# Two up-projection loads moved ahead of four modulation loads, and twelve PSUM copies moved from VectorE to ScalarE

## The chip, the cores and the metric

The kernel runs on one core of a Trainium2 chip. The metric is the device time of one execution in microseconds (us); it is the median over several executions of the same program. The engines are TensorE (PE in the rows; its weight loads are PEld), VectorE (DVE), ScalarE (ACT), GpSimd (POOL) and SyncE (SP), whose only work here is to issue DMAs.

## What is computed

The whole program is a mixer block followed by two transformer layers over 256 tokens of 1024 features, in fp32. The change lies in the first layer's attention, a latent attention with 8 heads, and touches the modulation that runs beside it. Cut to that:

```python
mod = (silu(c) @ mod_w[i] + mod_b[i]).reshape(B, 6, D)     # six rows of 1024 per layer
hin = x * (1.0 + mod[:, 1]) + mod[:, 0]

proj = hin @ w_in                                           # 1024 -> 576
c_q  = rms_norm(proj[..., :256], q_norm)
c_kv = rms_norm(proj[..., 256:512], kv_norm)
k_rope = apply_rope(proj[..., 512:], cos, sin)
q  = (c_q  @ w_uq ).reshape(B, S, 8, 192)                   # 128 plain + 64 rotary each
kv = (c_kv @ w_ukv).reshape(B, S, 8, 256)                   # 128 keys + 128 values each
q = concat([q[..., :128], apply_rope(q[..., 128:], cos, sin)])
k = concat([kv[..., :128], broadcast(k_rope)])
o = causal_softmax_attention(q, k, kv[..., 128:], 192 ** -0.5)
y = merge_heads(o) @ w_o
```

## The kernel before

Every large matmul is done in three passes: a weight `w` and an activation `x` are each split into a rounded part and a rest (`wh`, `wl`, `xh`, `xl`), and `wh*xh + wh*xl + wl*xh` accumulates in PSUM. `split` makes the two parts of a weight: a CAST on ScalarE (line 174) and a subtraction on VectorE (line 175). All weights stream from HBM through one pool of six tiles named `raw` (8 KB in each partition); a load can be issued only when one of the six is free again, and all loads are issued by SP in one order.

The attention function `mla` runs so. `tokens` and `halves` multiply the 256 tokens by `w_in` (tiles `ps_lat`, weights `lat0` to `lat7`), in two blocks of 128 tokens. `done(tb)` then normalises the 256+256 latents of a block: squares on ScalarE (`lsq`), a reciprocal square root on GpSimd (`lr`), two scalings on VectorE (`lt`, lines 1206 and 1207), five transposes on TensorE (`ltT`, `ltR`), and the split of the transposed latents into `ck` and `cq`, ScalarE and VectorE by turns. `units(0)` and `units(1)` are the up-projections, four heads each: a load of 1 MB of `w_ukv` (`raw_ukv`), four loads of together 768 KB of `w_uq` (`raw_uq`), the splits of both, the values (`ps_mlv`), the keys (`ps_kn`), the rotary part of the queries (`ps_qr`, then `rope`) and the plain part (`ps_qn`). The second half runs in pieces between the heads (`fill`). The three PSUM tiles of the tag "M" are used in turn by `ltT`, `ltR`, `mlv`, `kn`, `qr` and `qn`, so a tile that is copied out late holds up a later matmul.

The modulation is a queue of 48 load-and-multiply units of 1 MB each (`raw_mod`, `ps_mod`), four to a row of `mod`, with a closing step after each four that reads the sum (`modr`), transposes it (`modt`) and copies it out (`mod`). `halves` fetches `fill` units ahead of time and multiplies them after its own matmuls, while the normalisation runs. All units of a row share one PSUM tile (tag "V"), and the next row's can start only after the closing copy. In this attention the two last units of row 2 of the first layer's modulation and the four of the next row come up; the program's names for them are `mod044`, `mod046`, `mod030`, `mod032`, `mod034`, `mod036`.

What each engine does in which order is decided when the program is built: a scheduler orders the instructions of each engine by a model of their times, and the order is fixed from then on. Each engine runs its own list strictly in order and waits at semaphores.

Of the kernel before, what the change touches and what calls it, by code (L numbers as in the profile page):

```python
# [13 lines left out]
ALU = mybir.AluOpType  # L14
# [4 lines left out]
P = 128  # L19
S = 256  # L20
# [27 lines left out]
class G:  # L48
# [202 lines left out]
            for tb in range(2):  # L251
                self.nc.scalar.copy(out[tb][:, c:c + 512], pst[tb])

    def halves(self, load, ks, x, acc, width, name, ends, done=None, fill=0, by_column=False):

        ws = {}
        for i, k in enumerate(ks):
            with ExitStack() as ctx:  # L260
                if k != ends[0]:
                    self.after_marks(ctx)
                ws[k] = self.split(load(k), f"{name}{k}", i >= NW)
        self.fetch(fill)
        orders = []
        for tb in range(2):
            cols = list(enumerate(width[tb]))
            late = ks if by_column and tb else ks[-2:]
            orders.append([(k, n, c) for k in ks[:-len(late)] for n, c in cols] + [(k, n, c) for n, c in cols for k in late])
        ins = None  # L270
        for tb in range(2):
            t = slice(tb * P, (tb + 1) * P)
            with nullcontext() if ins is None or done is None else self.tc.issue_after(ins.ins):
                for k, n, c in orders[tb]:
                    wh, wl = ws[k]
                    ins = self.mm3t(acc(tb, n), x[k][0][:, t], x[k][1][:, t], wh[:, c], wl[:, c], k == ends[0], k == ends[1])
            if tb == 0:
                self.flush()
            if done is not None and tb == 0:
                done(0)  # L280
        if fill:
            with self.tc.issue_after(ins.ins):
                self.units(fill)
        if done is not None:
            self.pending = lambda: done(1)

    def tokens(self, w, x, groups, acc, done, name, c0=0, width=None, fill=0, by_column=False):

        width = (N512, TAIL) if by_column else (width or N512,) * 2
        load = self.loader(w, c0, width[0][-1].stop, name)  # L290
        for ks in groups:
            end = (done, fill, by_column) if ks is groups[-1] else ()
            self.halves(load, ks, x, acc, width, name, (groups[0][0], groups[-1][-1]), *end)

    def loader(self, w, c0, n, name):
# [892 lines left out]
def mla(g, x, ln, early):  # L1188
    nc, a = g.nc, g.a
    V, A, T = nc.vector, nc.scalar, nc.tensor  # L1190
    w = a["mla_w_in_2"][0]
    cuts = [slice(0, 256), slice(256, 576)]
# [4 lines left out]
    def done(tb):  # L1197
# [22 lines left out]
            V.scalar_tensor_tensor(l_[:, t], o, w_, h_[:, t].bitcast(F32), op0=ALU.mult, op1=ALU.subtract)  # L1220
        A.copy(kx[:, t], p2[:, 0:P])

    acc = lambda tb, n: lacc(tb, n, (256, 320)[n])
    g.tokens(w, x, [[0, 1, 2, 3], [4, 5, 6, 7]], acc, done, "lat", width=cuts, fill=6)
    g.flush()
    rest = early()

    def rope(src, name):
        ps = g.ps(name + "rp", "A")
        T.matmul(ps[:, 0:S], g.perm, src, start=True, stop=True)  # L1230
        t, u = g.t1(name + "rc"), g.t1(name + "rs")
        nc.gpsimd.tensor_tensor(t, src, g.trig[0], op=ALU.mult)
        V.tensor_tensor(u, ps[:, 0:S], g.trig[1], op=ALU.mult)
        nc.gpsimd.tensor_tensor(t, t, u, op=ALU.add)
        return t


    krr = rope(kx, "kr")
    kr = [g.t1(f"krz{e}") for e in range(2)]
    for e in range(2):  # L1240
# [5 lines left out]
    kn, qn = g.quad("kn0", F32) + g.quad("kn1", F32), g.quad("qn0", F32) + g.quad("qn1", F32)  # L1246

    def units(hf):
        rv = g.wload(a["mla_w_ukv_2"][0], 0, 2, 1024 * hf, 1024, f"ukv{hf}")
        raw = g.raw(f"uq{hf}")[:, 0:2 * 768].rearrange("p (k c) -> p k c", k=2)  # L1250
        for k in range(2):
            src = a["mla_w_uq_2"][0][k * P:(k + 1) * P, 768 * hf:768 * hf + 768].rearrange("p (h c) -> p h c", h=4)
            nc.sync.dma_start(raw[:, k, 0:512].rearrange("p (h c) -> p h c", h=4), src[:, :, 0:P])
            nc.sync.dma_start(raw[:, k, 512:768].rearrange("p (h c) -> p h c", h=4), src[:, :, P:192])
        with ExitStack() as ctx:
            if hf == 0:
                g.after_marks(ctx)
            ws = [g.split(rv[:, k, :], f"ukv{hf}{k}") for k in range(2)]
        wv = [[t.rearrange("p (h c) -> p h c", h=4) for t in w_] for w_ in ws]
        pv = [g.ps(f"mlv{hf}{tb}", "M") for tb in range(2)]  # L1260
        for tb in range(2):
            for k in range(2):
                t = slice(tb * P, (tb + 1) * P)
                o = pv[tb].rearrange("p (h c) -> p h c", h=4)
                g.mm3t(o, ck[k][0][:, t], ck[k][1][:, t], wv[k][0][:, :, P:S], wv[k][1][:, :, P:S], k == 0, k == 1)
            A.copy(vt[tb][:, 512 * hf:512 * hf + 512], pv[tb])
            yield
        for hh in range(4):
            h = 4 * hf + hh
            ps = g.ps(f"kn{h}", "M")  # L1270
            for k in range(2):
                g.mm3(ps[:, 0:S], wv[k][0][:, hh, 0:P], wv[k][1][:, hh, 0:P], *ck[k], k == 0, k == 1)
            A.copy(kn[h], ps[:, 0:S])
            yield
        with ExitStack() as ctx:
            if hf == 0:
                g.after_marks(ctx)
            wq = [g.split(raw[:, k, :], f"uq{hf}{k}") for k in range(2)]
        for pr in range(2):
            ps = g.ps(f"qr{hf}{pr}", "M")  # L1280
            for k in range(2):
                h_, l_ = (t[:, 512 + P * pr:512 + P * pr + P] for t in wq[k])
                g.mm3(ps[:, 0:S], h_, l_, *cq[k], k == 0, k == 1)
            xq = g.t1(f"qrx{hf}{pr}")
            V.tensor_copy(xq, ps[:, 0:S])
            yield
            qr[2 * hf + pr] = rope(xq, f"qr{hf}{pr}")
            for e in range(2):
                hh = 2 * pr + e
                h = 4 * hf + hh  # L1290
                ps = g.ps(f"qn{h}", "M")
                for k in range(2):
                    h_, l_ = (t[:, hh * P:hh * P + P] for t in wq[k])
                    g.mm3(ps[:, 0:S], h_, l_, *cq[k], k == 0, k == 1)
                ins = V.tensor_copy(qn[h], ps[:, 0:S])
                if hf and rest:
                    rest.pop(0)(ins)
                yield

    for _ in units(0):  # L1300
        pass
    later = units(1)

    def fill(st):
# [11 lines left out]
    n, done = ln()  # L1316
    acc = g.pair("mlay")
# [147 lines left out]
def program(tc, a, out):  # L1465
    with ExitStack() as ctx:
        g = G(ctx, tc, a)
        g.out = out
        g.wk = ctx.enter_context(tc.tile_pool(name="wk", bufs=1))
        h, hl, pw = block1(g)  # L1470
        n = gated(g, h, hl, pw)
        for i in range(2):
            def mid(i=i, n=n):
                g.bg_to(i, 3)
                return resid_ln(g, i, 0, n.r, (g.mod[i][4], g.mod[i][3]), f"ln{i}0")

            n = (mla, moba)[i](g, n.x, mid, n.residual)

            def end(i=i, n=n):
                g.bg_to(i, 5)  # L1480
                if i == 0:
                    g.bg_to(1, 0)
                    return resid_ln(g, 0, 1, n.r, (g.mod[1][1], g.mod[1][0]), "ln01")
                return None, last_ln(g, n.r)

            n = ffn(g, i, n.x, end, n.residual)
        g.flush()
# [32 lines left out]
```

## Time and profile before

| | |
|---|---|
| median of 3 runs | 877.22 us (877.14 to 877.37) |
| the profiled execution's own time | 879.18 us |
| its span, first to last instruction | 877.4 us |
| TensorE busy | 859.3 us, 98% of the span |
| VectorE busy / ScalarE busy | 673.2 us / 502.6 us |
| HBM traffic over the span | 226 GB/s |
| latent attention up to its output projection | about 270 to 343 us after the start |

The time of the profiled execution lies 1.8 us above its span, and the median of the runs 2.0 us below it; differences between stages are read in the span. A row of the timeline gives the start, the length, the engine, the line, the operation with its output and input tiles, how many instructions were merged, and in brackets how long the engine stood idle before it and whom it waited for. A length of a matmul includes its drain, so matmuls follow each other faster than their lengths.

### The profile page before, as it was taken

The numbers are of one execution on the slowest core, as the hardware profiler recorded it, in microseconds if no ns is written. First come the engines' busy times: TensorE is split into PE (matmuls) and PEld (weight loads), VectorE is DVE, ScalarE is ACT, GpSimd is POOL, SyncE is SP. The second block draws the span as 40 slices with busy tenths as digits, with TensorE's granted clock in tenths as the row PEclk, the third lists the DMA queues.
The fourth block names the chain that finished last, engine by engine and source line by source line (L and its number), as shares of the span: only waits on it lengthen the run. The fifth ranks groups of instructions, "written<-read, shape, count | busy, mean of one in ns | idle before, by whom it ended". The sixth has DMA issues, their size and how long they took to land. (4 is left out here: it accounts for less than half of the span.)

```text
span 877.4 us, 14288 instructions
## 1 busy us (share of the span) xinstructions
PE 859.3 (98%) x5415; PEld 741.1 (84%) x5415; DVE 673.2 (77%) x1289; ACT 502.6 (57%) x925; POOL 52.6 (6%) x81
## 2 busy tenths in 40 slices
PE   9999999999999899999999999999999999999996
PEld 8998779999888688798888888678888988888885
DVE  5798787768767576679899998675866686777786
ACT  6555666445557555377556557276553775565660
POOL 2003111000000131000000000000000000000003
PEclk9999999999999999999999999999999999999999
DMA  8955796854447963498898985498453956566411
GB/s 269 357 197 175 279 345 202 285 211 151 144 150 258 305 250 117 132 377 286 305 331 296 336 290 190 162 345 296 161 176 104 377 178 203 181 220 204 143 49 48
DMA packets 112760, 199.27 MB, mean 227 GB/s; under 512 B 8388, under 2 KB 76468, under 8 KB 112692
## 3 DMA queue, kind: packets, MB, share of 16 engines
q1 hardware_dynamic: 111892, 196.25, 65.7%
q0 software_dynamic: 496, 1.59, 0.5%
q8 instruction: 42, 0.69, 0.3%
q10 hardware_dynamic: 304, 0.53, 0.2%
q14 instruction: 26, 0.21, 0.1%
HBM read 197.28 MB, written 1.08 MB: 226 GB/s over the span
## 5 line engine op out<-in xcount | busy, mean ns | idle before, releaser
L194 PE MATMUL ps_f<-ln,wh_f 128*128 128x512 f32 x576 | 203.8, 396 | 0.0
L195 PE MATMUL ps_f<-ln,wl_f 128*128 128x256 f32 x576 | 161.4, 280 | 0.0
L194 PEld LDWEIGHTS ps_f<-ln,wh_f 128*128 128x128 f32 x576 | 108.1, 188 | 26.5 <-issue 0.8
L195 PEld LDWEIGHTS ps_f<-ln,wl_f 128*128 128x128 f32 x576 | 108.7, 189 | 1.4 <-issue 0.4
L174 ACT CAST wh_fo<-raw_fo 128x1024 fp32r<-128x1024 f32 x38 | 39.9, 1050 | 39.3 <-PE ps_f L194 38.2
L174 ACT CAST wh_f<-raw_fa 128x1024 fp32r<-128x1024 f32 x36 | 37.7, 1051 | 40.8 <-PE ps_f L194 20.3
L175 DVE TENSOR_TENSOR wl_fo<-raw_fo,wh_fo 128x1024 fp32r<-128x1024 f32 x38 | 46.5, 1223 | 19.0 <-ACT wh_fo L174 18.9
L175 DVE TENSOR_TENSOR wl_f<-raw_fa,wh_f 128x1024 fp32r<-128x1024 f32 x36 | 43.9, 1222 | 15.3 <-ACT wh_f L174 15.3
L174 ACT CAST wh_f<-raw_fb 128x1024 fp32r<-128x1024 f32 x36 | 37.1, 1050 | 28.0 <-PE ps_fy L215 17.8
L998 DVE SCALAR_TENSOR_TENSOR modacc<-raw_mod,c,modacc 128x1024 f32<-128x1024 f32 x40 | 51.1, 1278 | 2.0 <-ACT modacc L996 2.0
L175 DVE TENSOR_TENSOR wl_f<-raw_fb,wh_f 128x1024 fp32r<-128x1024 f32 x36 | 43.4, 1221 | 9.2 <-ACT wh_f L174 8.9
L188 PE MATMUL ps_fi<-ln,wh_fi 128*128 128x256 f32 x128 | 35.6, 285 | 0.0
L215 PE MATMUL ps_fy<-wh_fo,fh 128*128 128x512 f32 (+1 forms) x99 | 35.2, 369 | 0.0
L214 PE MATMUL ps_fy<-wl_fo,fh 128*128 128x512 f32 (+1 forms) x99 | 35.1, 368 | 0.0
L189 PE MATMUL ps_fi<-ln,wl_fi 128*128 128x256 f32 x128 | 34.6, 283 | 0.0
L187 PE MATMUL ps_fi<-ln,wh_fi 128*128 128x256 f32 x128 | 34.0, 286 | 0.0
L213 PE MATMUL ps_fy<-wh_fo,fh 128*128 128x512 f32 (+1 forms) x99 | 33.3, 367 | 0.0
L204 DVE TENSOR_TENSOR adf<-ps_f,adf 128x256 f32<-128x256 f32 x72 | 30.0, 417 | 0.0
L983 PE MATMUL ps_mod<-raw_mod,c 128*32 128x256 f32 x400 | 26.9, 383 | 1.0 <-DVE mod L1013 1.0
L203 ACT COPY adf<-ps_f 128x256 f32<-128x256 f32 x72 | 26.1, 363 | 0.0
L174 ACT CAST wh_fi<-raw_fi 128x1024 fp32r<-128x1024 f32 x16 | 17.0, 1079 | 14.9 <-PE ps_mlay L215 8.3
L188 PEld LDWEIGHTS ps_fi<-ln,wh_fi 128*128 128x128 f32 x128 | 24.5, 192 | 0.4 <-DVE ln L377 0.4
(807 smaller groups left out, 2582.4 us busy)
## 6 DMA issues: line engine op xcount, KB each, us to landing
raw_mod<-in_mod_w_dram SPq DMA_DIRECT2D x48, 1024.0 KB
raw_fo<-in_ffn_w_out_dram SPq DMA_DIRECT2D x22, 1024.0 KB
raw_fa<-in_ffn_w_in_dram SPq DMA_DIRECT2D x18, 1024.0 KB
raw_fb<-in_ffn_w_in_dram SPq DMA_DIRECT2D x18, 1024.0 KB
raw_fi<-in_ffn_w_in_dram SPq DMA_DIRECT2D x16, 512.0 KB
raw_wo<-in_w_out_dram SPq DMA_DIRECT2D x6, 1024.0 KB
raw_aqk<-in_w_in_dram SPq DMA_DIRECT2D x4, 1024.0 KB
raw_mqk<-in_w_in_dram SPq DMA_DIRECT2D x4, 1024.0 KB
```

Source lines behind the costliest of these rows:

```text
L174: self.nc.scalar.copy(hv, src)
L175: self.nc.vector.tensor_tensor(lv, src, hv.bitcast(F32), op=ALU.subtract)
L187: T.matmul(ps, wh, xh, start=start, stop=False, skip_group_check=chk)
L188: T.matmul(ps, wh, xl, start=False, stop=False, skip_group_check=chk)
L189: T.matmul(ps, wl, xh, start=False, stop=stop, skip_group_check=chk)
L194: T.matmul(ps, wh, x[2], start=start, stop=False, skip_group_check=True)
L195: T.matmul(ps[:, 0:S], wl, x[0], start=False, stop=stop, skip_group_check=True)
L204: V.tensor_tensor(t, ps[:, 0:S], t, op=ALU.add)
L213: T.matmul(ps, xh, wh, start=start, stop=False)
L214: T.matmul(ps, xh, wl, start=False, stop=False)
L215: return T.matmul(ps, xl, wh, start=False, stop=stop)
L998: nc.vector.scalar_tensor_tensor(st["acc"], rv[:, e], c, st["acc"], op0=ALU.mult, op1=ALU.add)
```

## The change

Three edits. The loads of an up-projection half become a function `loads(hf)`; for half 0 it is called from inside `halves` (argument `pre`), after the input projection's own loads and ahead of the fetch of modulation units, so these two tiles stand earlier in SP's order. Four units are fetched and multiplied there (`fill=4`) where there were six; the other two of the row are asked for later by `fill`'s call of `bg`. And the query tiles, rotary (`qrx`) and plain (`qn`), are copied out of PSUM by ScalarE where VectorE did it; the residual scalings that were pinned behind that copy are pinned behind a step of `rope` (`g.turn`).

```diff
-    def halves(self, load, ks, x, acc, width, name, ends, done=None, fill=0, by_column=False):
+    def halves(self, load, ks, x, acc, width, name, ends, done=None, fill=0, by_column=False, pre=None):
...
                 ws[k] = self.split(load(k), f"{name}{k}", i >= NW)
+        if pre is not None:
+            pre()
         self.fetch(fill)
...
+    def loads(hf):
+        rv = g.wload(a["mla_w_ukv_2"][0], 0, 2, 1024 * hf, 1024, f"ukv{hf}")
+        raw = g.raw(f"uq{hf}")[:, 0:2 * 768].rearrange("p (k c) -> p k c", k=2)
+        for k in range(2):
+            src = a["mla_w_uq_2"][0][k * P:(k + 1) * P, 768 * hf:768 * hf + 768].rearrange("p (h c) -> p h c", h=4)
+            nc.sync.dma_start(raw[:, k, 0:512].rearrange("p (h c) -> p h c", h=4), src[:, :, 0:P])
+            nc.sync.dma_start(raw[:, k, 512:768].rearrange("p (h c) -> p h c", h=4), src[:, :, P:192])
+        return rv, raw
...
-    g.tokens(w, x, [[0, 1, 2, 3], [4, 5, 6, 7]], acc, done, "lat", width=cuts, fill=6)
+    first = []
+    g.tokens(w, x, [[0, 1, 2, 3], [4, 5, 6, 7]], acc, done, "lat", width=cuts, fill=4, pre=lambda: first.append(loads(0)))
...
-        V.tensor_tensor(u, ps[:, 0:S], g.trig[1], op=ALU.mult)
+        g.turn = V.tensor_tensor(u, ps[:, 0:S], g.trig[1], op=ALU.mult)
...
     def units(hf):
-        rv = g.wload(...)          # and the raw_uq loads, as in loads() above
+        rv, raw = first.pop() if first else loads(hf)
...
-            V.tensor_copy(xq, ps[:, 0:S])
+            A.copy(xq, ps[:, 0:S])
...
-                ins = V.tensor_copy(qn[h], ps[:, 0:S])
+                A.copy(qn[h], ps[:, 0:S])
                 if hf and rest:
-                    rest.pop(0)(ins)
+                    rest.pop(0)(g.turn)
```

SP, the order of the loads behind the input projection's last one. Before, from the row's last two modulation units on (`ukv0`, `uq0` are the first half's up-projection weights, `ukv1`, `uq1` the second half's, `modb` the bias that a closing step adds):

```order
L159 DMA raw_mod034_3413<-in_mod_w_2_dram 128x2x1024
L159 DMA raw_mod036_3415<-in_mod_w_2_dram 128x2x1024
L159 DMA raw_ukv0_3558<-in_mla_w_ukv_2_dram 128x2x1024
L1253 DMA raw_uq0_3560<-in_mla_w_uq_2_dram 128x4x128
L1254 DMA raw_uq0_3560<-in_mla_w_uq_2_dram 128x4x64
L1253 DMA raw_uq0_3560<-in_mla_w_uq_2_dram 128x4x128
L1254 DMA raw_uq0_3560<-in_mla_w_uq_2_dram 128x4x64
L1005 DMA modb03_3970<-in_mod_b_2_dram 128x1x256
L159 DMA raw_ukv1_3716<-in_mla_w_ukv_2_dram 128x2x1024
```

Now, at the same place in SP's list (`ukv0`, `uq0`, `mod044` and `mod046` stand ahead of it, in that order):

```order
L159 DMA raw_mod030_3416<-in_mod_w_2_dram 128x2x1024
L159 DMA raw_mod032_3418<-in_mod_w_2_dram 128x2x1024
L159 DMA raw_ukv1_3712<-in_mla_w_ukv_2_dram 128x2x1024
L1231 DMA raw_uq1_3714<-in_mla_w_uq_2_dram 128x4x128
L1232 DMA raw_uq1_3714<-in_mla_w_uq_2_dram 128x4x64
L1231 DMA raw_uq1_3714<-in_mla_w_uq_2_dram 128x4x128
L1232 DMA raw_uq1_3714<-in_mla_w_uq_2_dram 128x4x64
L159 DMA raw_mod034_3919<-in_mod_w_2_dram 128x2x1024
L1007 DMA modb03_3970<-in_mod_b_2_dram 128x1x256
L159 DMA raw_mod036_3959<-in_mod_w_2_dram 128x2x1024
```

The first half's weights have gone ahead of the modulation, the second half's weights have taken their old place, and `mod034` and `mod036` stand behind the second half's weights.

TensorE, after the input projection (`ltT`, `ltR` transposes of the latents, of block 0 and 1; `modt` the closing step's transposes; `mlv` the values). Before:

```order
L1215 MATMUL ps_ltR0_3455<-ident_88,lt0_3449 128x128
L1215 MATMUL ps_ltT1_3523<-ident_88,lt1_3518 128x128 x4
L1011 MATMUL ps_modt04_3767<-ident_88,modr04_3763 128x128 x2
L983 MATMUL ps_mod03_3772<-raw_mod030_3409,c_774 32x256 x8
L983 MATMUL ps_mod03_3772<-raw_mod032_3411,c_774 32x256 x8
L983 MATMUL ps_mod03_3772<-raw_mod034_3413,c_774 32x256 x8
L983 MATMUL ps_mod03_3772<-raw_mod036_3415,c_774 32x256 x8
L1215 MATMUL ps_ltR1_3524<-ident_88,lt1_3518 128x128
L213 MATMUL ps_mlv00_3573<-wh_ukv00_3565,ckh0_3227 128x512
```

Now:

```order
L1013 MATMUL ps_modt04_3763<-ident_88,modr04_3759 128x128 x2
L985 MATMUL ps_mod03_3768<-raw_mod030_3416,c_774 32x256 x8
L985 MATMUL ps_mod03_3768<-raw_mod032_3418,c_774 32x256 x8
L1217 MATMUL ps_ltT1_3526<-ident_88,lt1_3521 128x128 x4
L1217 MATMUL ps_ltR1_3527<-ident_88,lt1_3521 128x128
L213 MATMUL ps_mlv00_3569<-wh_ukv00_3561,ckh0_3227 128x512
L214 MATMUL ps_mlv00_3569<-wl_ukv00_3562,ckh0_3227 128x512
L215 MATMUL ps_mlv00_3569<-wh_ukv00_3561,ckl0_3228 128x512
L213 MATMUL ps_mlv00_3569<-wh_ukv01_3565,ckh1_3229 128x512
L214 MATMUL ps_mlv00_3569<-wl_ukv01_3566,ckh1_3229 128x512
L215 MATMUL ps_mlv00_3569<-wh_ukv01_3565,ckl1_3230 128x512
L985 MATMUL ps_mod03_3768<-raw_mod034_3919,c_774 32x256 x8
```

`mod034` now stands behind the six matmuls of the first value tile, and `mod036` further down, behind the first two key tiles (not shown).

VectorE, after the scaling of block 0 (`lt0`) up to the scaling of block 1 (`lt1`). Before:

```order
L1207 TENSOR_SCALAR lt0_3449<-ps_lat00_3252,lr0y_3446 128x256
L1203 TENSOR_SCALAR lss1_3510<-lss1_3510 128x2
L325 TENSOR_SCALAR lr1y_3515<-lss1_3510 128x2
L1206 TENSOR_SCALAR lt1_3518<-ps_lat11_3363,lr1y_3515 128x256
L1207 TENSOR_SCALAR lt1_3518<-ps_lat10_3359,lr1y_3515 128x256
L1008 SCALAR_TENSOR_TENSOR modr04_3763<-ps_mod04_3206,modb04_3764 128x256
```

Now:

```order
L1209 TENSOR_SCALAR lt0_3452<-ps_lat00_3252,lr0y_3449 128x256
L175 TENSOR_TENSOR wl_ukv00_3562<-raw_ukv0_3405,wh_ukv00_3561 128x1024
L175 TENSOR_TENSOR wl_ukv01_3566<-raw_ukv0_3405,wh_ukv01_3565 128x1024
L175 TENSOR_TENSOR wl_uq00_3618<-raw_uq0_3407,wh_uq00_3617 128x768
L1205 TENSOR_SCALAR lss1_3513<-lss1_3513 128x2
L1010 SCALAR_TENSOR_TENSOR modr04_3759<-ps_mod04_3206,modb04_3760 128x256
L175 TENSOR_TENSOR wl_uq01_3622<-raw_uq0_3407,wh_uq01_3621 128x768
L1222 SCALAR_TENSOR_TENSOR ckl0_3228<-ps_ltT0_3457,cols1_756,ckh0_3227 128x128
L327 TENSOR_SCALAR lr1y_3518<-lss1_3513 128x2
L1015 COPY mod04_3766<-ps_modt04_3763 128x2x4
```

The four subtractions of the first half's weights have moved ahead of block 1's normalisation and of the closing step of the modulation row.

## Rows read from the trace of the kernel before

**Rows 1.** The page, part 1: busy time and share of each engine.

```profile
PE 859.3 (98%) x5415; PEld 741.1 (84%) x5415; DVE 673.2 (77%) x1289; ACT 502.6 (57%) x925; POOL 52.6 (6%) x81
```

**Rows 2.** Waits of TensorE: who for whom, total us, times, longest.

```profile
PE ps_mlv L213 <- ACT krx L1221: 2.6, 1, 2.6
...
PE ps_qn L187 <- DVE qn L1295: 1.3, 2, 0.7
...
PE ps_qr11rp L1230 <- DVE qrx L1285: 0.5, 1, 0.5
```

**Rows 3.** Stretches: length, busy per engine, granted clock, DMA share, GB/s.

```profile
291.50:297.10 5.60, 4.91 (x71) 2.54 (x70) 3.03 (x12) 2.51 (x10) 0.00 (x0) 1.00 1.02 305
297.10:300.50 3.40, 1.20 (x5) 0.76 (x5) 2.33 (x3) 3.40 (x7) 0.00 (x0) 0.98 0.92 257
...
300.00:303.00 3.00, 3.00 (x9) 2.14 (x8) 3.00 (x6) 1.13 (x3) 1.76 (x4) 0.56 1.07 349
303.00:306.00 3.00, 3.00 (x20) 2.69 (x19) 0.63 (x3) 1.80 (x5) 0.88 (x1) 0.88 1.13 309
...
327.00:330.00 3.00, 1.84 (x14) 1.42 (x12) 3.00 (x9) 1.94 (x6) 1.16 (x2) 1.00 0.47 108
```

**Rows 4.** SP's timeline, 289 to 295 us: three of the loads.

```profile
289.91 0.37 SPq L159 DMA_DIRECT2D raw_ukv<-in_mla_w_ukv_dram  x1
...
292.98 1.54 SPq L1254 DMA_DIRECT2D raw_uq<-in_mla_w_uq_dram  x1
294.62 0.75 SPq L1005 DMA_DIRECT2D modb<-in_mod_b_dram  x1
```

**Rows 5.** ScalarE's timeline, 297 to 324 us.

```profile
297.09 1.99 ACT L174 CAST wh_ukv<-raw_ukv 128x1024 fp32r<-128x1024 f32 x2 [2.53 <-DMA raw_ukv<-in_mla_w_ukv_dram]
...
306.91 0.37 ACT L1273 COPY kn<-ps_kn 128x256 f32<-128x256 f32 x1 [0.29 <-PE ps_kn L189]
307.31 2.00 ACT L174 CAST wh_ukv<-raw_ukv 128x1024 fp32r<-128x1024 f32 x2
...
322.08 1.98 ACT L174 CAST wh_mlay<-raw_mlay 128x1024 fp32r<-128x1024 f32 x2
```

**Rows 6.** VectorE's timeline, 288 to 312 us.

```profile
288.85 0.47 DVE L1207 TENSOR_SCALAR lt<-ps_lat,lr0y 128x256 f32<-128x256 f32 x1
...
289.81 0.17 DVE L325 TENSOR_SCALAR lr1y<-lss 128x2 f32<-128x2 f32 x1
290.79 0.48 DVE L1206 TENSOR_SCALAR lt<-ps_lat,lr1y 128x256 f32<-128x256 f32 x1 [0.81 <-POOL lr1y L327]
...
291.58 0.41 DVE L1008 SCALAR_TENSOR_TENSOR modr<-ps_mod,modb 128x256 f32<-128x256 f32 x1
...
298.17 2.36 DVE L175 TENSOR_TENSOR wl_ukv<-raw_ukv,wh_ukv 128x1024 fp32r<-128x1024 f32 x2 [3.23 <-ACT wh_ukv L174]
...
301.04 1.05 DVE L175 TENSOR_TENSOR wl_uq<-raw_uq,wh_uq 128x768 fp32r<-128x768 f32 x1
...
311.82 0.41 DVE L1295 COPY qn<-ps_qn 128x256 f32<-128x256 f32 x1
```

**Rows 7.** TensorE's timeline, 288 to 315 us.

```profile
288.78 1.93 PE L983 MATMUL ps_mod<-raw_mod,c 128*32 128x256 f32 x32
...
292.75 3.66 PE L983 MATMUL ps_mod<-raw_mod,c 128*32 128x256 f32 x64 [0.26 <-DVE mod L1013]
...
299.30 0.50 PE L213 MATMUL ps_mlv<-wh_ukv,ckh 128*128 128x512 f32 x1 [2.63 <-ACT krx L1221]
...
304.37 0.28 PE L187 MATMUL ps_kn<-ckh,wh_ukv 128*128 128x256 f32 x1
...
313.68 0.48 PE L213 MATMUL ps_mlv<-wh_ukv,ckh 128*128 128x512 f32 x1
314.00 0.39 PE L214 MATMUL ps_mlv<-wl_ukv,ckh 128*128 128x512 f32 x1
314.23 0.40 PE L215 MATMUL ps_mlv<-wh_ukv,ckl 128*128 128x512 f32 x1
```

More of the change, by code (lines that the diff above doesn't have):

```diff
@@ L285, in halves, with tokens @@
             self.pending = lambda: done(1)
-    def tokens(self, w, x, groups, acc, done, name, c0=0, width=None, fill=0, by_column=False):
+    def tokens(self, w, x, groups, acc, done, name, c0=0, width=None, fill=0, by_column=False, pre=None):
         width = (N512, TAIL) if by_column else (width or N512,) * 2
@@ L291, in tokens @@
         for ks in groups:
-            end = (done, fill, by_column) if ks is groups[-1] else ()
+            end = (done, fill, by_column, pre) if ks is groups[-1] else ()
             self.halves(load, ks, x, acc, width, name, (groups[0][0], groups[-1][-1]), *end)
@@ L1248, in units @@
     def units(hf):
[L1249 to L1254, printed above, removed]
+        rv, raw = first.pop() if first else loads(hf)
         with ExitStack() as ctx:
```

## The prediction

> **What bounds the kernel now.** I first read the page's busy shares: TensorE is busy 98% of the span and every other engine far less [rows 1]. So an edit pays only where it takes idle or slowed time out of TensorE, and work moved between VectorE and ScalarE pays only through what TensorE waits for. Next, TensorE's waits: at this stage they are one of 2.6 us ahead of the values (`mlv`), two for a query tile's PSUM (`qn`, 1.3 together, the longer 0.7), and one of 0.5 for a rotary query (`qr11rp`) [rows 2].
>
> The first is named after `krx`, but the reader should see in ScalarE's timeline that this engine itself sat 2.53 us for the DMA of `ukv0` and began the cast at 297.09 [rows 5]; the values followed at 299.30 after 2.63 us of idle TensorE [rows 7]. SP had issued that load only at 289.91, 7.2 us before the cast [rows 4]: its slot came free when TensorE had multiplied `mod044` (the stretch from 288.78, [rows 7]).
>
> The stretches show a second cost behind the first. TensorE was busy 1.20 of 3.40 us between 297.1 and 300.5; then the granted clock read 0.56 in 300 to 303 and 0.88 in 303 to 306, with TensorE busy throughout [rows 3]. With a part h of a stretch at half speed the clock reads 1 - h/2, so 0.88 of the first 3 us and 0.24 of the next were at half, 2.64 + 0.72 = 3.4 us, in which half the work was lost: 1.7 us. So this load costs 2.6 + 1.7 = 4.3 us before; the waits of the second half cost 1.8 more and no clock: the stretch 327 to 330, with TensorE busy 1.84 of 3.00, kept 1.00 [rows 3].
>
> By the Trainium skill, "TensorE: Matmul & The Clock Gate", section "HAM oscillation — how this bites in real kernels", gaps in which matmuls wait for a DMA send the clock to half, and the work behind the gap pays for it; the 0.56 of [rows 3] agrees.
>
> **The change, part by part.** Differences are in the span of the profiled execution (877.4) and are added to the median of the runs, 877.22; that execution's own time lay 2.0 above the median, which cancels.
>
> *Early loads.* The number of issues is the same and they run on SP. `ukv0` and `uq0` now land behind the input projection's weights, so the 2.63 us wait goes. But the bytes up to the end of the row are the same, and something else takes their place: `ukv1` stands where `ukv0` was (issue at 289.91, on the same release by `mod044`), the four pieces of `uq1` where those of `uq0` were, and `mod034` where the small `modb` was, 294.62 [rows 4]. `mod034`'s slot is that of `ukv0`, free after VectorE's second subtraction, which is earlier (291.6, below).
>
> *The normalisation's wait.* VectorE's four subtractions for `ukv0` and `uq0` have moved ahead of the second block's normalisation and of the closing step. From the end of `lt0` at 289.3: two of `ukv` 2.36, one of `uq` 1.05 (as at 298.17 and 301.04), then `modr04` 0.41, the second `uq` 1.05: 294.2 at the soonest, and `lr1y` only then, where it ran at 289.81 [rows 6]. Queued behind are `modt04`, its copy, `mod030` and `mod032` on TensorE: they start near 294.7 instead of 292.75 [rows 7], with some 3 us of idle TensorE in pieces of about 0.5 to 1.2 between 291 and 294.7. A unit of the modulation takes 3.66 / 4 = 0.92 [rows 7], so the two end at 296.6; then the transposes of block 1, whose scaled latents (`lr1y` plus 0.98 to the scaling, 0.48 each, [rows 6]) are there by 296.2, and six `mlv` matmuls at 0.23, 1.4 us [rows 7]. With about 0.7 for the five transposes and the splits between (my estimate), TensorE stands before `mod034` at 298.7. Those 3 us cost nothing as long as `mod034` lands later than that.
>
> *When does `mod034` land?* `ukv0` took 7.2 us from issue to cast [rows 4, 5]; the same from 294.62 gives 301.8. By bytes: behind 291.5 come `ukv1` 1.05 MB, `uq1` 0.79 and `mod034` 1.05, 2.88 MB; 305 GB/s carry 1.71 by 297.1, 257 carry 0.87 by 300.5, the last 0.30 at 349 take 0.9: 301.4 [rows 3]. Below: if the queue, never empty now, moved 400 GB/s after 297.1 (above any stretch shown, so a bound), 2.9 us, 300.0. Above: by bytes `ukv0` would have been there at 291.5 + 1.05 MB / 305 GB/s = 294.9, and it came 2.2 later; with that on top of 301.4, 303.6. I take 301.8, the lag of the nearest like load. TensorE then idles 301.8 - 298.7 = 3.1 us, slightly more than the 2.63 of before.
>
> *From there to the second half's first values* (313.68 before). Before, 313.68 - 304.37 = 9.3 us ran from the first key matmul [rows 7]. Now, behind the landing: those 9.3, plus `mod034` and `mod036` 1.83, the other six `mlv` matmuls 1.4, the rotary keys' matmul 0.3 (a 128x256 matmul, 0.28), minus a `qn` wait of 0.6 that the new copies remove, plus 0.3 (next paragraph): 12.5. 301.8 + 12.5 = 314.3, or +0.6.
>
> *Copies on ScalarE.* Twelve copies at 0.41 leave VectorE, 4.9 us [rows 6], and twelve at 0.37, 4.4 us, come to ScalarE [rows 5], both engines with room in the average. What counts is the queue. Gone are the waits behind VectorE's chains: 0.6, 0.7 and 0.5 [rows 2]. New: in the first half a query copy stands behind both casts of the second half's `wh_ukv` (2.00 us from 307.31); PSUM's other two tiles cover six matmuls each of 0.12 (half of 0.23, half the columns), so of 2.00 + 0.37, less the 0.45 until the tile is full and 1.6 of cover, 0.3 is left. In the second half a key copy and a query copy stand behind the two `wh_mlay` casts, 1.98 + 0.36 - 1.4 = 0.9 [rows 5]. Sum of the second half: -0.7 - 0.5 + 0.9 = -0.3. Its bounds are -1.2 (casts fall in a gap) and +1.1 (both copies caught in full).
>
> By the Trainium skill, "ScalarE: Activation LUTs", section "Rules for kernel authors", simple element-wise work belongs on VectorE, up to about 3 times as fast in bf16. By that these copies would cost ScalarE near 15 us against 5, not 4.4; the fp32 copies out of PSUM here show 0.41 and 0.37, so the trace doesn't agree.
>
> *At nothing:* the residual scalings are pinned elsewhere but nothing of TensorE waits for them in this stage; if it did, one scaling of about 1 us would be its price. The modulation's row closes later, used first by the output's residual, tens of us on.
>
> **Sum, at a full clock:** +0.6 - 0.3 = +0.3, 877.5. **If the clock halves again** behind the stall as it did in [rows 3], the same 3.4 us at half cost +1.7 (before's own loss is already in the 313.68): +2.0, 879.2.
>
> **The rivals.**
> - **A, forecast:** the wait moves from the values to `mod034`, 3 us, and the clock halves after it. For: the stall is as long as the one that was followed by 0.56. The bytes and the slots are the same. 879.2, own range 878.0 to 880.4.
> - **B, the same stall, clock kept:** for: in 327 to 330 TensorE idled 1.16 of 3.00 in pieces and the clock stayed at 1.00 [rows 3]; against: this stall is one piece. 877.5, own range 876.4 to 878.4.
> - **C, the load comes in time:** `mod034` lands by 300.0. Stall 1.3, no halving; 300.0 + 12.5 = 312.5, -1.2 against 313.68, and ScalarE's casts fall in a gap, -1.2: 874.8. It decides once the landing lies under about 300.5. For it: SP no longer stands between 284 and 289.9, so the queue isn't empty. Against: 257 to 349 GB/s in every stretch here. This is the faster side, and the one in which the change does what its move suggests.
> - **D, later still:** landing at 303.6, +1.8 on A, or ScalarE's queue takes the +1.1: 880.8.
> - **E, nothing at TensorE's end:** the two loads were hidden anyway. Against: a wait of 2.53 on that very DMA [rows 5]; no chance worth a number.
>
> **How the numbers follow.** A 0.49, B 0.30, C 0.13, D 0.08. This kernel's runs can tell about 0.2% from no change, 1.75 us: 875.5 and 879.0. C lies under that; D above it; A is cut by 879.0, some 0.29 above and 0.20 below; nearly all of B lies within. Faster 0.13, same 0.50, slower 0.37. Predicted: A's 879.2. 876.2 leaves C out, 0.13, and 880.6 most of D, about 0.06, which is what the range may lose.
>
> **What would show it.** Right: no wait for `raw_ukv`; one for `raw_mod` of 2.5 to 3.5 us before a `ps_mod` matmul near 298.7, then a granted clock near 0.6 over 3 us; small waits at `modt` and `ps_mod` near 292 to 294.7; waits for `qn` or `kn` copies on ScalarE in place of VectorE's. Wrong: if `mod034` is there when TensorE comes (C); if the idle pieces of 291 to 294.7 alone halve the clock, so that TensorE comes to `mod034` late and the loss is hidden; or if the second half's waits grow past 1 us.

## The result and the profile after

The changed kernel takes 881.98 us (median of four executions, 881.05 to 883.52) against 877.22 before: ratio 1.0053, 95% interval 1.0038 to 1.0068. It is slower by half a per cent, on the forecast side, but 2.8 us beyond the forecast and above the range.

In the profiled execution after (881.05, span 879.3), every step of the forecast can be found. The waits of TensorE between 285 and 345 us (who for whom, total us, times, longest):

```profile
PE ps_mod L985 <- DMA raw_mod<-in_mod_w_dram: 2.9, 1, 2.9
PE ps_qn L187 <- ACT kn L1281: 1.4, 2, 1.0
PE ps_modt L1013 <- DVE modr L1010: 1.0, 1, 1.0
PE ps_mod L985 <- DVE mod L1015: 0.8, 1, 0.8
PE ps_mlao L1184 <- ACT mlapT L1179: 0.6, 1, 0.6
PE ps_ltR L1217 <- ACT lt L1213: 0.3, 1, 0.3
```

The wait for the values [rows 2] is gone, and one of the same size stands ahead of a modulation unit. TensorE's timeline shows where, and what comes behind it:

```profile
288.69 1.93 PE L985 MATMUL ps_mod<-raw_mod,c 128*32 128x256 f32 x32
...
292.85 0.44 PE L1013 MATMUL ps_modt<-ident,modr 128*128 128x128 f32 x2 [1.01 <-DVE modr L1010]
294.12 1.93 PE L985 MATMUL ps_mod<-raw_mod,c 128*32 128x256 f32 x32 [0.83 <-DVE mod L1015]
...
296.79 0.50 PE L213 MATMUL ps_mlv<-wh_ukv,ckh 128*128 128x512 f32 x1
...
301.31 1.07 PE L985 MATMUL ps_mod<-raw_mod,c 128*32 128x256 f32 x16 [2.86 <-DMA raw_mod<-in_mod_w_dram]
...
316.01 0.48 PE L213 MATMUL ps_mlv<-wh_ukv,ckh 128*128 128x512 f32 x1
```

The values start at 296.79 where they started at 299.30 [rows 7]; then `mod034` waits 2.86 us for its DMA; and the second half's values start at 316.01, 2.3 us later than in [rows 7]. The reason for the pieces of idle time at 292.85 and 294.12 is in VectorE's timeline, where the subtractions for `ukv0` and `uq0` stand ahead of `modr` and `lr1y`:

```profile
289.17 2.35 DVE L175 TENSOR_TENSOR wl_ukv<-raw_ukv,wh_ukv 128x1024 fp32r<-128x1024 f32 x2
291.44 0.95 DVE L175 TENSOR_TENSOR wl_uq<-raw_uq,wh_uq 128x768 fp32r<-128x768 f32 x1
292.31 0.16 DVE L1205 TENSOR_SCALAR lss<-lss 128x2 f32<-128x2 f32 x1
292.38 0.42 DVE L1010 SCALAR_TENSOR_TENSOR modr<-ps_mod,modb 128x256 f32<-128x256 f32 x1
...
293.84 0.16 DVE L327 TENSOR_SCALAR lr1y<-lss 128x2 f32<-128x2 f32 x1
```

SP's timeline has `ukv1` in the old place of `ukv0` [rows 4], and `mod034` behind the pieces of `uq1`, landing 8.1 us after its issue:

```profile
289.82 0.37 SPq L159 DMA_DIRECT2D raw_ukv<-in_mla_w_ukv_dram  x1
...
293.25 2.13 SPq L159 DMA_DIRECT2D raw_mod<-in_mod_w_dram  x1
```

And the stretches (length, busy per engine, granted clock, DMA share, GB/s) show the clock at half behind the wait:

```profile
300.50:303.00 2.50, 1.69 (x19) 1.05 (x19) 0.00 (x0) 0.00 (x0) 0.00 (x0) 0.93 1.02 309
303.00:306.00 3.00, 3.00 (x9) 2.39 (x8) 0.42 (x1) 0.90 (x3) 0.73 (x1) 0.50 1.02 404
```

So profile against profile the change costs 881.05 - 879.18 = 1.87 us, where 2.0 were forecast. The medians differ by 4.8 us. The question for the experiments is where the other 2.9 come from, besides whether the steps are causes.

### The profile page after: what moved, and what is told of

It is laid out like the page before. It is cut to its first block, busy times and chain, and to the rows that moved or that the text cites. A ratio compares the mean times of both kernels' runs of the same rounds, so it can differ in the third digit from the quotient of the medians.

```text
span 879.3 us, 14284 instructions
## 1 busy us (share of the span) xinstructions
PE 858.7 (98%) x5415; PEld 740.3 (84%) x5415; DVE 669.8 (76%) x1277; ACT 506.5 (58%) x937; POOL 52.3 (6%) x81
```

## The experiments

Each kernel was run several times beside the kernel before, on one chip for each set. "Mean clock" is that of one execution. It can be read roughly. In all eleven profiles of this case the clock also reads half at the end of the span, where TensorE has no work left; that costs no time and takes 1.6 to 2.9 us' worth of clock, as here in the profile of the first experiment:

```profile
870.00:872.00 2.00, 0.00 (x0) 0.00 (x0) 1.97 (x5) 0.00 (x0) 0.13 (x1) 0.50 0.00 0
```

A half-clock stretch in which TensorE works took 1.7 us each time that a profile shows one. So by my estimate 0.997 or more has no room for such a stretch, 0.995 or 0.996 means one, and 0.994 or less more than one. Where in the program it lay, only a profile tells.

**The kernel before, again.** 

> The kernel before, unchanged, to read the clock and the span of several executions, not of one. Theory (clock): the profiled execution of before, 879.18, had a half-clock stretch behind the 2.63 us wait, and the timed ones, 877.22, had none; so some executions show a span near 875.4 and a mean clock of about 0.998, others 877.4 and 0.996. Rival (the 2.0 us is only what surrounds a profiled execution): all executions show about the same mean clock, 0.996, and the same span, whatever their time.

Measured: eleven executions, median 877.31; of them six at 876.88 to 877.31 with mean clocks of 0.997 or 0.998, five at 877.88 to 878.54, three of these with 0.996. The profiled one took 876.89, span 875.1, 2.3 us less than the one that the forecast was made from. ScalarE's cast, TensorE's values, a key tile, the second half's values, and two stretches in it:

```profile
295.34 1.99 ACT L174 CAST wh_ukv<-raw_ukv 128x1024 fp32r<-128x1024 f32 x2 [0.92 <-DMA raw_ukv<-in_mla_w_ukv_dram]
```

```profile
297.55 0.50 PE L213 MATMUL ps_mlv<-wh_ukv,ckh 128*128 128x512 f32 x1 [1.01 <-ACT krx L1221]
...
304.33 0.39 PE L187 MATMUL ps_kn<-ckh,wh_ukv 128*128 128x256 f32 x1 [0.70 <-ACT kn L1273]
...
311.41 0.48 PE L213 MATMUL ps_mlv<-wh_ukv,ckh 128*128 128x512 f32 x1
```

```profile
297.00:300.00 3.00, 2.45 (x10) 1.82 (x11) 2.09 (x4) 2.36 (x6) 1.09 (x3) 1.00 0.96 289
300.00:303.00 3.00, 3.00 (x23) 2.77 (x22) 2.96 (x6) 1.21 (x3) 1.53 (x2) 1.00 1.13 318
```

The same load landed 1.75 us sooner (295.34 for 297.09), the wait was 1.01 for 2.63, and no half clock followed; of the 1.62 + 1.7 saved, 0.70 went into a wait for a key tile, and the second half's values came 2.27 us sooner (the 0.35 between wasn't traced). The theory holds as far as one more profile and the mean clocks go: what the first profile showed as the price of the kernel isn't in the execution at the median, which reads 0.998. Whether the three at 0.996 paid it at the same place isn't known; the copies alone, below, show another place.

**The changed kernel, again.** 

> The changed kernel, unchanged, to read the wait, the clock and the span of several executions. Theory (its wait for mod034 is there in every execution and the clock halves behind it in every one): all executions at 881 to 884, mean clocks of 0.994 to 0.996, none under 880. Rival (as in the kernel before, only some executions are caught): some executions at 879 or less with a mean clock of 0.997 or more.

Measured: six executions, 880.43 to 884.26, median 882.18 (before beside it 877.50; ratio 1.0055, interval 1.0038 to 1.0072), mean clocks 0.992 to 0.996. None is spared, so the rival falls. But the theory, too, is right only for the wait and the times: in the profiled execution the half clock came sooner, behind the pieces of idle time at 292.9 and 294.1, and the wait for `mod034`, to which TensorE then came at 301.97 - 2.45 = 299.52, covered it:

```profile
294.00:297.00 3.00, 2.87 (x28) 1.38 (x32) 2.18 (x9) 1.56 (x6) 0.70 (x1) 0.51 1.12 318
```

```profile
301.97 1.07 PE L985 MATMUL ps_mod<-raw_mod,c 128*32 128x256 f32 x16 [2.45 <-DMA raw_mod<-in_mod_w_dram]
```

That execution is the shortest of the six, 880.43.

**One part of the change alone.** The loads alone, with the query tiles on VectorE:

```diff
-            A.copy(xq, ps[:, 0:S])
+            V.tensor_copy(xq, ps[:, 0:S])
...
-                A.copy(qn[h], ps[:, 0:S])
+                ins = V.tensor_copy(qn[h], ps[:, 0:S])
...
```

> The change without the copies on ScalarE: loads early and four units fetched, query tiles copied by VectorE. Theory (the wait for mod034 and the clock behind it carry the loss, the copies give back about 0.3): 882 to 883 in most executions, a wait of about 2.9 us for mod034 at 301 and a granted clock near 0.5 behind it. Rival (the copies on ScalarE carry the loss): within 1 us of before, 876 to 878.

And the copies alone, the same lines the other way in the kernel before: 

> The kernel before with the query tiles copied by ScalarE and nothing else changed. Theory: within 1 us of before, 876.2 to 877.5, the three waits of the second half exchanged for others. Rival (the copies carry the loss): 879 or more, with waits on ScalarE of more than 1 us that before doesn't have.

Measured: the loads alone 884.35 (five executions, 882.17 to 884.89; ratio 1.0073, interval 1.0061 to 1.0085); the copies alone 877.22 against 877.63, ratio 0.9996, interval 0.9987 to 1.0004. So all of the loss is in the loads and the units. The loads alone came out above the 882 to 883 expected, and 2.2 us above the changed kernel, measured on another chip; the intervals against before overlap, so this isn't settled. Their profiled execution has the wait for `mod034` at 4.25 us and a half clock behind it, and another half clock 120 us ahead of this stage, at a place that none of the edits touches:

```profile
180.00:183.00 3.00, 3.00 (x17) 2.47 (x16) 2.04 (x7) 1.33 (x2) 0.00 (x0) 0.78 1.02 395
183.00:186.00 3.00, 3.00 (x19) 3.00 (x19) 0.94 (x1) 0.00 (x0) 0.00 (x0) 0.65 0.70 287
```

The profile of the copies alone (877.97, mean clock 0.995) has the one half clock in which TensorE works at the same place, with TensorE busy throughout ahead of it. In the stage of the change it has none, and the wait for the values, with the loads in the old order, is again the short one:

```profile
177.00:180.00 3.00, 3.00 (x22) 2.47 (x20) 2.01 (x5) 0.00 (x0) 0.00 (x0) 1.00 0.24 73
180.00:183.00 3.00, 3.00 (x16) 2.47 (x15) 2.04 (x7) 1.33 (x2) 0.00 (x0) 0.79 0.98 385
183.00:186.00 3.00, 3.00 (x20) 3.00 (x19) 0.86 (x1) 0.00 (x0) 0.00 (x0) 0.65 0.70 287
```

```profile
299.40 0.50 PE L213 MATMUL ps_mlv<-wh_ukv,ckh 128*128 128x512 f32 x1 [1.26 <-ACT krx L1221]
```

So a low mean clock in a run without a trace needn't come from this stage. The copies are worth little: from the second half's first values to the output projection it took 29.61 us in the changed kernel, 29.79 with the loads alone, and 29.81 and 29.82 in the two profiles of the kernel before.

**The units held back on TensorE.** Loads and SP's order as in the changed kernel; `mod034` and `mod036` are multiplied behind the key tiles and behind the second query tile:

```diff
...
+            hold = None
+            if not g.early:
+                g.fetch(1)
+                hold = g.hold.pop(0)
+            with nullcontext() if hold is None else g.tc.issue_after(hold.ins):
                 g.bg()
```

> The changed kernel, with the multiplications of mod034 and mod036 held back on TensorE behind the key tiles and behind the second query tile; the loads' order on SP is as in the changed kernel. Theory (the place of mod034 in TensorE's order is what costs): no wait of over 1 us for a modulation load, no half clock in this stage, 874 to 876, under before. Rival (another transfer or ScalarE is late next, and the wait goes there): a new wait of 2 to 3 us ahead of the keys or queries, 879 or more.

Measured: 877.01 (twelve executions) against 877.63, ratio 0.9994, interval 0.9985 to 1.0003. About 5 us of the change's cost are gone by moving the small matmuls of two units. But the median isn't clear of before, and not at the 874 to 876 of the theory: half of the executions lie at 876.10 to 876.46, the other half at 877.55 to 878.90 with mean clocks of 0.995 or 0.996, and the profiled one is of the latter:

```profile
304.68 1.07 PE L985 MATMUL ps_mod<-raw_mod,c 128*32 128x256 f32 x16
```

```profile
294.00:297.00 3.00, 3.00 (x32) 1.24 (x32) 1.96 (x7) 1.31 (x6) 0.55 (x1) 0.50 1.10 295
```

No wait stands ahead of `mod034`. In this profile the pieces of idle time between 291 and 294 now cost what they are, with a half clock behind them.

**The units ahead of the second half's weights on SP.** `fill=6` in place of `fill=4`: 

> The changed kernel with six units fetched and multiplied as before (the loads of the first half still ahead of them), so that mod034 and mod036 stand ahead of ukv1 and uq1 on SP. Theory (mod034's landing follows its place among the bytes): the wait for mod034 falls under 1.5 us, a wait for mod036 of about 2 us takes part of its place, 878 to 880. Rival (the landing hangs on the slot or on something else): the same wait near 301 as in the changed kernel, 881 to 884.

Measured: 879.24 (twelve executions) against 877.50, ratio 1.0017, interval 1.0009 to 1.0026. No wait for a modulation load is left, neither for `mod034` nor, against the expectation, for `mod036`. With six units `mod034` also stands ahead of the values on TensorE. That doesn't explain the missing wait, since TensorE came to it no later than in the changed kernel: the row below holds the 32 matmuls of `mod030` and `mod032` and the first 6 of `mod034`, and it ends at 298.48. So the landing follows the place among the bytes.

```profile
294.61 3.87 PE L985 MATMUL ps_mod<-raw_mod,c 128*32 128x256 f32 x38 [0.83 <-DVE mod L1015]
```

What the profile still shows are the pieces of idle time (1.0 and 0.8) and a half clock behind them, 0.71 and 0.72 in the stretches 294 to 297 and 297 to 300. The half clock isn't all that is left of the loss: six of the twelve executions have 0.997 or 0.998 and still take 878.46 to 879.71.

**Work in the place of the wait.** 26 matmuls into the unused half of `mod034`'s PSUM tile, ahead of it:

```diff
...
+                    for _ in range(FILLER):
+                        with g.tc.issue_after(g.hold.ins):
+                            g.hold = T.matmul(st["full"][:, S:2 * S], g.idle[0], g.idle[1], start=True, stop=True, skip_group_check=True)
...
```

> The changed kernel with 26 matmuls of 128x256 put on TensorE between the first value tile and mod034, about 3 us of work that nobody needs, into the unused half of mod034's PSUM tile; the order of everything else is that of the changed kernel. Theory (the clock falls because TensorE stands idle, and costs 1.7 us of its own behind the wait): no half clock at 301 to 306, and 1.5 to 2 us less than the changed kernel beside it. Rival (the wait alone costs, or the clock falls for another reason): the same time as the changed kernel within 0.7 us, or more.

Measured: 880.92 (six executions) against 882.18 of the changed kernel on the same chip, 1.3 less, between the 1.5 to 2 of the theory and the 0.7 of the rival; the intervals against before (1.0021 to 1.0048 and 1.0038 to 1.0072) overlap, so the size isn't settled. The clock is: five of six executions have 0.997 or more, where none of the ten of the changed kernel has, and in the profiled one both stretches that follow read 1.00, though `mod034` landed so late there that 1.45 us of waiting were left:

```profile
300.00:303.00 3.00, 2.10 (x17) 1.84 (x15) 0.43 (x1) 0.81 (x2) 0.73 (x1) 1.00 1.02 351
303.00:306.00 3.00, 2.45 (x22) 1.65 (x23) 0.00 (x0) 0.00 (x0) 0.00 (x0) 1.00 1.01 371
```

```profile
303.55 1.07 PE L987 MATMUL ps_mod<-raw_mod,c 128*32 128x256 f32 x16 [1.45 <-DMA raw_mod<-in_mod_w_dram]
```

**The second block first.** The units held back further (behind the second and fourth query tile), and VectorE's subtractions behind the second block's normalisation and the closing step:

```diff
...
-        if tb == 0:
-            g.marks = [ia, iv]
+        g.marks = [ia, iv]
...
+    g.fetch(1)
+    g.marks = [g.closed, g.parts[0]]
+    g.units(2)
...
```

> The kernel of the units held back, and in addition VectorE's work in another order: the second block's normalisation and the closing step of the modulation row go ahead of the subtractions for ukv0 and uq0, and mod034 and mod036 are multiplied behind the second and fourth query tile. Theory (the idle pieces between 291 and 294.7 cost once mod034's wait no longer covers them): their sum falls under 1.5 us, no half clock there, 873 to 875, under every execution of the kernel before. Rival (the subtractions are then late for the values and the wait only moves): a wait of 1.5 us or more ahead of mlv or kn, 876 to 878.

Measured: 877.54 (twelve executions, eleven of them at 0.997 or 0.998) against 877.50, ratio 0.9999, interval 0.9991 to 1.0007. No half clock is left in the stage, the pieces sum to 1.25 (0.29, 0.43, 0.24 and 0.29), and the time is the rival's nonetheless, with a wait of 1.14 us ahead of a key tile (1.5 was its condition). ScalarE's timeline offers a reason, the copies to `krz`, waiting for GpSimd, in front of the copies of the values:

```profile
300.83 0.82 ACT L1259 COPY krz<-krrc 64x256 f32<-64x256 f32 x2 [1.88 <-POOL krrc L1250]
301.67 1.07 ACT L1277 COPY mlav<-ps_mlv 128x512 f32<-128x512 f32 x2
```

and VectorE's shows the second block's start held by squares that stood behind casts on ScalarE:

```profile
291.25 0.17 DVE L1205 TENSOR_SCALAR lss<-lss 128x2 f32<-128x2 f32 x1 [1.29 <-ACT lsq L1203]
```

**Both queues mended.**

```diff
...
-    g.marks = [g.closed, g.parts[0]]
+    g.marks = [g.msq, g.mcopy, g.closed, g.parts[0]]
...
+            if (hf, tb) == (0, 1):
+                with g.tc.issue_after(ins.ins):
+                    for e in range(2):
+                        A.copy(kr[e][64 * e:64 * e + 64, :], krr[64 * e:64 * e + 64, :])
...
```

> The kernel with the second block first, and two more places: ScalarE's casts of ukv0 stand behind the second block's squares and those of uq0 behind the copies of krx, and the two copies to krz stand behind the copies of the values. Theory (the 1.14 us wait of a key tile was for a value copy queued behind krz, and the 1.29 us of VectorE ahead of lss for squares queued behind casts): both waits under 0.4 us, 875.5 to 876.5, about 1 us under the kernel before. Rival (a further copy or subtraction is late next): the same 877 to 878 with a new wait of about 1 us.

Measured: 875.39 (twelve executions, 874.88 to 876.87) against 877.49, ratio 0.9971, interval 0.9960 to 0.9982: faster than before by 2.1 us, a little more than expected, and than the changed kernel, over the medians of different sets, by some 6.6. All that is left of waits between 285 and 345:

```profile
PE ps_qn L187 <- ACT kn L1289: 1.0, 2, 0.5
PE ps_mlao L1184 <- ACT mlapT L1179: 0.6, 1, 0.6
PE ps_ltR L1218 <- DVE cql L1223: 0.3, 1, 0.3
PE ps_mod L985 <- DVE mod L1015: 0.3, 1, 0.3
```

Both waits that were to go are gone (the one ahead of a key tile, and VectorE's ahead of `lss` is 0.28). The rows sum to 2.2 us; those of the kernel with the second block first sum to 4.0. So TensorE waits 1.8 us less, and the median fell by 2.1, from 0.04 above before to 2.10 under it. Which of the two edits gave how much wasn't tried apart.

## Why the prediction was wrong

**The wait that moves: right.** TensorE came to `mod034` at 301.31 - 2.86 = 298.45 (forecast 298.7) and the load was there at 301.31 (301.8). That this agrees so well is partly luck: SP issued the load at 293.25 and not at 294.62, and it took 8.1 us and not 7.2, two misses that nearly cancel. That the place among the bytes and the place in TensorE's order make this wait is shown by the kernels with six units and with the units held back: the first takes it away although TensorE comes no later, the second with SP's order unchanged.

**The half clock behind it: right in kind and size in the profiled execution.** 0.93 over 2.5 us and 0.50 over 3 make (0.07 x 2.5) + (0.50 x 3) = 1.7 us lost. In the other profile of the changed kernel the idle pieces alone halved the clock and the wait hid it, which the prediction had named as a sign of being wrong; so "behind it" holds in one profile of two. That the half clock goes when work fills the wait is shown by the filler; how much of the median it is, 1.3 us there, isn't settled. And idle time isn't the only occasion: at 180 to 186 it came in two profiles without any.

**The normalisation's wait: right, with its condition.** 0.30, 1.01 and 0.83 in place of pieces summing to 3. "Those 3 us cost nothing as long as `mod034` lands later than that" was borne out both ways: the pieces are hidden in the changed kernel, and paid, with a half clock, in the profile with the units held back.

**The second half: right.** The keys' and queries' waits on ScalarE are 0.39 and 0.98 (forecast 0.3 and 0.9); a wait of 0.56 for `mlapT` wasn't foreseen. From the second half's values to the output projection 0.2 us are won (29.61 for 29.81), for a forecast of 0.3. That the copies might be dearer on ScalarE finds no support: they took 0.37 to 0.39 us there, for 0.41 on VectorE, and moving them alone changed nothing that can be measured.

**The step that failed** is the price of before: "this load costs 2.6 + 1.7 = 4.3 us", read from one profile and set off in full against the new wait and half clock, with the profile's distance from the median put aside as "2.0 above the median, which cancels". It doesn't cancel. The 2.0 were not something around the execution: the profiled execution itself was 2.3 us longer in the span than the one profiled later (877.4 for 875.1), by that very wait and half clock. In that later profile, which lies 0.3 us under the median of the runs before, the load cost a wait of 1.01 us, no half clock, and 0.70 at a key tile. (What lies around the span is the same in both kernels, 879.18 - 877.4 = 1.78 and 881.05 - 879.3 = 1.75.) So there was little to win and as much to lose as forecast. Against the later profile the steps give 879.3 - 875.1 = 4.2 us, and with it 877.22 + 4.2 = 881.4, within 0.6 of what was measured. All of it has arisen by the output projection, which starts 4.4 us later than in that profile (below, the profile of before taken later and the one after); in the second profile of the changed kernel it starts at 344.73, 3.5 later, of 878.7 - 875.1 = 3.6 in the span.

```profile
341.23 0.48 PE L213 MATMUL ps_mlay<-wh_mlay,mlao 128*128 128x512 f32 x1
345.62 0.47 PE L213 MATMUL ps_mlay<-wh_mlay,mlao 128*128 128x512 f32 x1
```

**What stays open:** the last 0.6 to 0.9 us. The profiled execution of the changed kernel is the shortest of its four, and the two longest, 882.71 and 883.52, have a mean clock of 0.994 for 0.996. By the estimate above 0.994 is more than one half-clock stretch, and a second one of 1.7 us (as at 180 to 186 in the loads alone) would make up 882.71 from 881.05. A later `mod034` (4.25 us of waiting there) could add to it. Neither of the two left a trace, so this isn't shown. Nor is the reason why the load of `ukv0` landed 1.75 us apart in the two profiles of before.

## What to carry to other kernels

A profile is one execution: when its time lies above the median by about as much as a term of the sum (here 2.0 us against a half clock of 1.7), that term may not be in the median at all, and what an edit removes there is not won. A load that is moved ahead puts others behind it; follow the bytes to the one that is now last, and look where its consumer stands in TensorE's order, since holding that consumer back was worth 5 us here, and the early loads without the wait brought nothing that can be measured. And when a wait goes, read the queue of the engine that is next: the version that beats both kernels needed, on top of the units held back and VectorE's work reordered, two copies and a few casts moved from in front of something urgent.

## What the runs showed of the hardware

The landing of one load, issued at the same point of the program (289.91 and 289.76), differed by 1.75 us between two executions of the same kernel. And equal idle time didn't always bring the half clock: the changed kernel has the same pieces (1.01 and 0.83 us) in both its profiles, and the clock in the stretch behind them, 294 to 297, reads 1.00 in one and 0.51 in the other. Nor did the half clock always need idle time: in two of eleven profiles it came at 180 to 186, with TensorE by the profile busy 3.00 of 3.00 us in each stretch from 171 on, and took 1.7 us there as everywhere; in the other nine the same stretches read 1.00.
